# Attention with one more unit in flight, and two tiles that share the late slices at the head of three phases

## The chip, the cores and the metric

The kernel runs on one core of one Trainium2 chip, as one launch. The metric is device time in microseconds (us): the median of the runs of a kernel. Below, PE is TensorE (PEld its weight loads), DVE is VectorE, ACT is ScalarE, POOL is GpSimd, SP is the queue that issues the transfers.

## The reference

One inference step of a two-layer backbone, `D_MODEL` 1024, for 512 latent tokens and 128 context tokens that share one set of weights. Layer 0 mixes by attention (4 query heads, 2 key and value heads of 128) beside a Hyena convolution, layer 1 by a bidirectional mLSTM. Each layer ends with a gated ConvFFN of width 2816. Queries are taken in blocks of 128 rows. Around every sub-layer stand RMSNorm and a modulation whose vectors come from `w_mod`.

```python
def block_attention(q, k, v):
    ...
    s = jnp.einsum('bqkgd,bskd->bkgqs', qi, kf) * scale
    p = jax.nn.softmax(s, axis=-1)
    return jnp.einsum('bkgqs,bskd->bqkgd', p, vf)
...
def conv_ffn(x, w_up, conv_w, conv_b, w_down):
    h = dwconv3(x @ w_up, conv_w, conv_b)
    return (jax.nn.gelu(h[..., :D_FF], approximate=False) * h[..., D_FF:]) @ w_down
...
for l in range(DEPTH):
    ...
    xs = xs + mod_s[2] * rms_norm(out_s, norm_mix_post[l])
    hs = modulate(xs, norm_ffn_pre[l], mod_s[3], mod_s[4])
    ...
```

The outputs are the new token states of both groups, the new keys and values of the context, and the mLSTM states.

## The kernel before

The 640 tokens are five tiles of 128: tiles 0, 1, 2 are the first half (384 columns), tiles 3 and 4 the second (256). Every large product is made of three matmuls of float32 halves, a high part h and a low part l (`mm3`): h by h, l by h, h by l. So each activation slice has two tiles (`a1h`, `a1l`; `a3h`, `a3l` in the second ConvFFN) and each weight tile three: the raw one from the transfer (`wr`), the high part cast by ACT (`wh`) and the rest subtracted by DVE (`wl`). There are three buffers of `wh` and `wl`. A weight tile is 128 output columns by 1024, that is eight slices of the contraction (`KT` = 8), so a slice on one half is three matmuls.

The order of the instructions on every engine is fixed when the program is built. A planner (`Order`, `od`) keeps a model of every engine; generators for side work are spawned with a lead, and the main list of tasks takes a step of them where its model finds room. `od.until` waits in the model until operands are there, `od.take` and `od.gave` count PSUM tiles. There are three PSUM tiles of 1024 columns ("mm") and two of 512 ("aux").

**The head of a phase** (`fm_head`, from line 447). A phase's activations come from the residual stream by norm, transposes and casts, eight slices one after the other. The first five weight tiles of a phase do the first half of the tokens (`early`), the later halves follow (`late`, in the rows `g00l`, `g10l`). Two early tiles share one PSUM tile, under one name in the rows. In the rows `u` at the start of a ConvFFN is the PSUM tile of specs 3 and 4: its weights are w33 and w34 in the first ConvFFN and w165 and w166 in the second. Tile 1 of a phase does slices 0 to 7 and waits for each, then tile 2 does slices 0 to 7. In the second ConvFFN slices 4 to 7 are still being made when tile 1 starts; their casts run on ACT, DVE and POOL (`o1p0nt` is the transpose, `o1p0ny` the modulated slice). The same boundary then makes the slices of the second half (`o1p3...`), while tile 3 and its successors run. The mLSTM phase has the same head with its own specs.

**Attention** (`attend`, from line 1455). A unit is a block i of 128 query rows and one head (kv head kv, one of its two query heads a): `s` holds the scores (512 new keys and 128 cached ones) in a PSUM tile "mm", DVE takes the maximum `mx`, ACT the exponential `p` with its sum, DVE the reciprocal `rr` and the scaling of p; PE transposes p in five pieces into another "mm" tile `pt`, which ACT copies to SBUF; PE multiplies by the values into an "aux" tile `po`, which ACT copies to `mx`h, the mixer's output page. There are 20 units; the four with i = 4 are the context's and have one key block instead of five. A unit may start when all but the three ahead of it have ended. In between, the last pieces of the Hyena convolution (`iy`, `iz`), of the key and query transposes (`qkt`) and, on DVE, the sums of `w_mod` (`acc`<-`mw`) are worked on. The output projection follows (`o`, weights w25 to w32).

Of the kernel before, what the change touches and what calls it, by code (L numbers as in the profile page):

```python
# [15 lines left out]
ALU = mybir.AluOpType  # L16
AX = mybir.AxisListType

P = 128
# [306 lines left out]
def hybrid_step(ctx: ExitStack, tc: tile.TileContext, A: dict, O: dict):  # L326
# [18 lines left out]
    def page(name, dt=F32):  # L345
        return pp.tile([P, 648], dt, tag="pg", name=name)
# [85 lines left out]
    def fm_task(src, act, name, evac, needs=()):  # L432
# [11 lines left out]
                yield  # L444
        return Task(run, src)

    def fm_head(specs, act, needs_a, needs_b):


        n_ = len(specs)  # L450
        specs = specs[3:] + specs[:3]
        st, left = {}, {}

        def early(n):
            def run(w):
                if n % 2 == 0:
                    od.take("mm")
                    st[n] = mm(specs[n][1])
                    left[n] = min(2, n_ - n)
                st[n, "w"] = w  # L460
                o = n % 2 * 512
                yield from fm_part(st[n - n % 2][:, o : o + CUT], w, act, 0, CUT, needs_a if n == 0 else None)
                if EVF:
                    yield
            return Task(run, specs[n][0], hold=n >= n_ - 3)

        def late(n):
            def run(w):
                m, o = n - n % 2, n % 2 * 512
                own = OWN and n == n_ - 1 and not o  # L470
                if own:
                    pl = st[m][:, 512:1024]
                else:
                    od.take("aux")
                    pl = aux(specs[n][1] + "l")
                held = w is None
                yield from fm_part(pl[:, 0 : T - CUT], st[n, "w"] if held else w, act, CUT, T,
                                   needs_b if n == back[0] else None)
                if held and RB:
                    if EVF:  # L480
                        yield
                    release()
                specs[n][2]([(st[m][:, o : o + CUT], 0, CUT), (pl[:, 0 : T - CUT], CUT, T)])
                if not own:
                    od.gave("aux", pl)
                left[m] -= 1
                if not left[m]:
                    od.gave("mm", st[m])
                if held and not RB:
                    release()  # L490
            return Task(run, None if n >= n_ - 3 else specs[n][0])

        back = list(range(max(0, n_ - 3), n_)) + list(range(max(0, n_ - 3)))
        return [early(n) for n in range(n_)] + [late(n) for n in back]
# [596 lines left out]
    def forward(src, cols, out, name):  # L1091
# [21 lines left out]
            diff.append(t)  # L1113
            yield
        (c, s), (dc, ds) = sums, diff
        for o, x, y, op in ((out[0][:, a], c[:, a], c[:, b], ALU.add), (out[0][:, b], c[:, a], c[:, b], ALU.subtract),
                            (out[1][:, a], s[:, a], s[:, b], ALU.add), (out[1][:, b], s[:, b], s[:, a], ALU.subtract),
                            (out[2][:, a], dc[:, a], ds[:, b], ALU.add),
                            (out[2][:, b], dc[:, a], ds[:, b], ALU.subtract),
                            (out[3][:, a], dc[:, b], ds[:, a], ALU.subtract),  # L1120
                            (out[3][:, b], dc[:, b], ds[:, a], ALU.add)):
            nc.vector.tensor_tensor(o, x, y, op=op)
        yield

    def filters():
        z, w = hy["z"], hy["w"]
# [160 lines left out]
    def long_conv(hf):  # L1287
# [15 lines left out]
        HYE.tensor_tensor(yp[:, h1], vp[:, h0], gi, op=ALU.mult)  # L1303
        nc.vector.tensor_tensor(vp[:, h0], vp[:, h1], gi, op=ALU.mult)
        HYE.tensor_tensor(vp[:, h1], vp[:, h1], gr, op=ALU.mult)
        nc.vector.tensor_tensor(yp[:, h0], yp[:, h0], vp[:, h0], op=ALU.subtract)
        nc.vector.tensor_tensor(yp[:, h1], yp[:, h1], vp[:, h1], op=ALU.add)
        yield
# [5 lines left out]
        for n in range(2):  # L1314
# [2 lines left out]
            HYE.tensor_tensor(x[1], S, gs, op=ALU.mult)  # L1317
            nc.vector.tensor_tensor(C, C, gs, op=ALU.mult)
            HYE.tensor_tensor(S, S, gc, op=ALU.mult)
            nc.vector.tensor_tensor(x[0], x[0], x[1], op=ALU.subtract)  # L1320
            nc.vector.tensor_tensor(C, C, S, op=ALU.add)
            pl, mi = page(f"vp{n}{hf}")[:, 0:512], page(f"vm{n}{hf}")[:, 0:512]
            a, b = slice(0, 256), slice(256, 512)

# [101 lines left out]
        od.ready.add(("qk", i))  # L1426

    scale = DH ** -0.5

    def scores(kv, i, a):  # L1430
        h, nm = 2 * kv + a, f"{2 * kv + a}{i}"
# [18 lines left out]
    def attend():  # L1450
# [31 lines left out]
        def unit(n, u):  # L1482
            kv, i, a = u
            nk = 5 if i < 4 else 1
            yield [("qk", j) for j in (range(4) if i < 4 else (4,))] + [("at", j) for j in range(n - 3)]
            yield "mm"
            p, su, rr = scores(*u)
            yield
            nc.vector.reciprocal(rr, su)
            nc.vector.tensor_scalar(p, p, rr, None, op0=ALU.mult)  # L1490
            yield
            yield "mm"
            transposed(u, p)
            yield
            yield "aux"
            values(u)
            od.ready.add(("at", n))
# [553 lines left out]
    def release(away=False):  # L2051
        state["live"] -= not away
        issue(state["split"] + state["raws"])
        prefetch()
# [217 lines left out]
```

## Time and profile before

| | |
|---|---|
| runs | 1753.57, 1753.31, 1750.95 us; median 1753.31 |
| the profiled execution's own time | 1750.03 us |
| its span | 1748.1 us |
| busy: PE, PEld | 1686.0 (96%), 1524.9 (87%) |
| busy: DVE, ACT, POOL | 1246.7 (71%), 747.0 (43%), 354.2 (20%) |
| mean granted clock of PE, as a share of full speed | 0.986 |
| HBM over the span | 114 GB/s |

The times in the rows are microseconds from the start of the span of one profiled execution. Busy is the time in which an engine had an instruction under way; PE's matmuls overlap, so that the distance of their starts is the better measure of what one costs. "Idle before" is how long an engine stood still ahead of a row, and "<-" names what was last to release it.

### The profile page before, as it was taken

How to read it: one execution, taken by the hardware profiler on the slowest of the kernel's cores; microseconds unless marked ns; L12 is line 12 of the kernel's file. 1: busy time of each engine (PE TensorE's matmuls, PEld its weight loads, DVE VectorE, ACT ScalarE, POOL GpSimd, SP SyncE). 2: the span in 40 equal slices, each digit the busy share in tenths (PEclk: the TensorE clock that was granted, in tenths of full speed). 3: DMA queues.
4: the chain of work that ended last, by engine and by line, in shares of the span. 5: the costliest groups of instructions: out<-in, count | busy, mean ns of one | idle time of the engine just before them, and what ended most of it. 6: DMA issues, size and time to landing. Idle time of an engine off the chain costs nothing. (4 is left out here: it accounts for less than half of the span.)

```text
span 1748.1 us, 25489 instructions
## 1 busy us (share of the span) xinstructions
PE 1686.0 (96%) x10074; PEld 1524.9 (87%) x10074; DVE 1246.7 (71%) x2057; ACT 747.0 (43%) x1233; POOL 354.2 (20%) x187
## 2 busy tenths in 40 slices
PE   7899998899999999999999999998999999999997
PEld 2678787779999999888899999996889999998886
DVE  4688796767878777987767888886578844445455
ACT  2422545545434344454555444334354422333343
POOL 0000121001546453431013211120014411111000
PEclk9999999999999999999999999998999999999999
DMA  9245122411434343463524212122114322223343
GB/s 344 103 151 169 46 90 100 138 68 61 160 132 144 133 145 125 157 214 121 181 93 147 71 55 80 59 70 100 49 63 155 121 73 76 81 73 109 125 160 125
DMA packets 64352, 203.85 MB, mean 117 GB/s; under 512 B 7335, under 2 KB 12455, under 8 KB 64234
## 3 DMA queue, kind: packets, MB, share of 16 engines
q1 hardware_dynamic: 64234, 202.23, 33.9%
q8 instruction: 79, 1.29, 0.3%
q14 instruction: 39, 0.32, 0.1%
HBM read 196.17 MB, written 3.94 MB: 114 GB/s over the span
## 5 line engine op out<-in xcount | busy, mean ns | idle before, releaser
L284 DVE TENSOR_TENSOR wl<-wr,wh 128x1024 fp32r<-128x1024 f32 (+1 forms) x260 | 317.4, 1225 | 111.1 <-ACT wh L284 111.0
L284 ACT CAST wh<-wr 128x1024 fp32r<-128x1024 f32 (+1 forms) x260 | 263.5, 1018 | 151.6 <-PE dn L365 108.1
L284 DVE SCALAR_TENSOR_TENSOR acc<-mw,sc,acc 128x1024 f32<-128x1024 f32 x91 | 169.8, 1883 | 3.9 <-DMA mw<-in_w_mod 3.6
L284 POOL TENSOR_TENSOR hid<-zg,zu 128x640 f32<-128x640 f32 x44 | 105.9, 2408 | 321.7 <-DVE zu L284 317.9
L284 POOL TENSOR_TENSOR acc<-acc,modp 128x1024 f32<-128x1024 f32 x49 | 146.1, 2981 | 115.2 <-ACT modp L284 91.1
L284 DVE SCALAR_TENSOR_TENSOR zg<-g,vec,zg 128x127 f32<-128x127 f32 (+3 forms) x168 | 87.4, 541 | 93.2 <-ACT zg L284 90.2
L365 PE MATMUL dn<-wh,hh 128*128 128x512 f32 x440 | 139.3, 397 | 1.8 <-DVE zu L284 1.6
L365 PE MATMUL dn<-wl,hh 128*128 128x512 f32 x440 | 138.2, 394 | 0.0
L365 PE MATMUL dn<-wh,hl 128*128 128x512 f32 x440 | 138.2, 394 | 0.0
L284 DVE SCALAR_TENSOR_TENSOR zu<-u,vec,zu 128x511 f32<-128x511 f32 (+2 forms) x164 | 86.7, 549 | 62.8 <-ACT zu L284 59.9
L284 ACT ACTIVATE zu<-u,vec 128x640 f32<-128x640 f32 (+1 forms) x42 | 36.8, 876 | 174.3 <-PE u L365 174.3
L365 PE MATMUL u<-a3h,wh 128*128 128x384 f32 (+1 forms) x336 | 104.8, 312 | 2.9 <-DVE a3h L284 1.5
L365 PE MATMUL u<-a3l,wh 128*128 128x384 f32 (+1 forms) x336 | 105.0, 313 | 0.3 <-POOL a3l L284 0.3
L365 PE MATMUL u<-a3h,wl 128*128 128x384 f32 (+1 forms) x336 | 104.7, 312 | 0.2 <-DVE wl L284 0.2
L365 PE MATMUL u<-a1l,wh 128*128 128x384 f32 (+1 forms) x336 | 104.4, 311 | 0.5 <-POOL a1l L284 0.5
L365 PE MATMUL g<-a1h,wh 128*128 128x384 f32 (+1 forms) x336 | 104.8, 312 | 0.0
L365 PE MATMUL u<-a1h,wh 128*128 128x384 f32 (+1 forms) x336 | 104.6, 311 | 0.1
L365 PE MATMUL g<-a3h,wh 128*128 128x384 f32 (+1 forms) x336 | 104.4, 311 | 0.0
L365 PE MATMUL u<-a1h,wl 128*128 128x384 f32 (+1 forms) x336 | 104.0, 310 | 0.2 <-DVE wl L284 0.2
L365 PE MATMUL g<-a3l,wh 128*128 128x384 f32 (+1 forms) x336 | 104.2, 310 | 0.0
L365 PE MATMUL g<-a1l,wh 128*128 128x384 f32 (+1 forms) x336 | 104.2, 310 | 0.0
L365 PE MATMUL g<-a3h,wl 128*128 128x384 f32 (+1 forms) x336 | 104.1, 310 | 0.0
(742 smaller groups left out, 4454.9 us busy)
## 6 DMA issues: line engine op xcount, KB each, us to landing
wr<-in_w_up SPq DMA_DIRECT2D x92, 512.0 KB, 3.3
wr<-in_w_down SPq DMA_DIRECT2D x82, 512.0 KB, 3.8
mw<-in_w_mod SPq DMA_DIRECT2D x80, 512.0 KB, 4.3
wr<-in_w_ml SPq DMA_DIRECT2D x34, 512.0 KB, 3.9
wr<-in_w_out SPq DMA_DIRECT2D x18, 512.0 KB, 3.9
wr<-in_w_in SPq DMA_DIRECT2D x13, 512.0 KB
wr<-in_w_u SPq DMA_DIRECT2D x12, 512.0 KB, 5.5
we<-in_w_mod SPq DMA_DIRECT2D x8, 512.0 KB, 8.0
```

The costliest lines, as they stand in the source:

```text
L284: r = f(*args, **kw)
L365: r = nc.tensor.matmul(out, lhsT, rhs, start=start, stop=stop)
```

## The change

Two parts change the order of the instructions, and no instruction is added or taken away.

In `attend` the distance after which a unit may start becomes a number, `ATW` = 4 where a literal 3 stood: a unit may start when all but the four ahead of it have ended.

In `fm_head` the first two tiles of a phase (`EM` = 2) do slices 0 to 4 (`EK` = 5) of tile 1, then 0 to 4 of tile 2, then 5 to 7 of tile 1, after which its weight buffer is released, then 5 to 7 of tile 2 and its release. The planner now waits for each slice of an early tile where it waited for two at once from the second tile on. `FINE` = 0 in the convolution's generators adds hooks that do nothing (left out below).

```diff
--- before.py
+++ after.py
@@ -444,6 +444,9 @@
                 yield
         return Task(run, src)
 
+    EM = 2
+    EK = 5
+
     def fm_head(specs, act, needs_a, needs_b):
 
 
@@ -452,17 +455,35 @@
         st, left = {}, {}
 
         def early(n):
+            m = EM if n < EM else 1
+
+            def part(i, w, ks):
+                o = i % 2 * 512
+                out = st[i - i % 2][:, o : o + CUT]
+                for k in ks:
+                    if i < EM:
+                        od.need([(*needs_a, k)])
+                    od.until(od.avail([x[:, k * P : (k + 1) * P] for x in w] + [x[:, 0:CUT] for x in act[k]]))
+                    mm3(out, [x[:, k * P : (k + 1) * P] for x in w], [x[:, 0:CUT] for x in act[k]], k == 0, k == KT - 1)
+                    if k % 2:
+                        yield
+
             def run(w):
                 if n % 2 == 0:
                     od.take("mm")
                     st[n] = mm(specs[n][1])
                     left[n] = min(2, n_ - n)
                 st[n, "w"] = w
-                o = n % 2 * 512
-                yield from fm_part(st[n - n % 2][:, o : o + CUT], w, act, 0, CUT, needs_a if n == 0 else None)
-                if EVF:
-                    yield
-            return Task(run, specs[n][0], hold=n >= n_ - 3)
+                if m == 1:
+                    yield from part(n, w, range(KT))
+                    return
+                yield from part(n, w, range(EK))
+                if n == m - 1:
+                    for i in range(m):
+                        yield from part(i, st[i, "w"], range(EK, KT))
+                        release()
+                yield
+            return Task(run, specs[n][0], hold=n >= n_ - 3 or m > 1)
 
         def late(n):
             def run(w):
...
@@ -1426,6 +1457,7 @@
         od.ready.add(("qk", i))
 
     scale = DH ** -0.5
+    ATW = 4
 
     def scores(kv, i, a):
         h, nm = 2 * kv + a, f"{2 * kv + a}{i}"
@@ -1482,7 +1514,7 @@
         def unit(n, u):
             kv, i, a = u
             nk = 5 if i < 4 else 1
-            yield [("qk", j) for j in (range(4) if i < 4 else (4,))] + [("at", j) for j in range(n - 3)]
+            yield [("qk", j) for j in (range(4) if i < 4 else (4,))] + [("at", j) for j in range(n - ATW)]
             yield "mm"
             p, su, rr = scores(*u)
             yield
```

On SP and POOL the order stays as it was. It moves on PE, DVE and ACT in the attention and in the three heads, and nowhere else.

**PE, start of the attention.** Rows with `s` are scores, `qkt` and `iz` leftovers of the keys and the convolution, `pt` transposes of p, `po` the product with the values (vv); the three digits are kv, i, a, those behind `s` the head and i. Before:

```order
L365 MATMUL s11_2232<-qkT4_1127,qkT1_1124 128x512
L365 MATMUL s11_2232<-kc_1129,qkT1_1124 128x128
L376 MATMUL qkt41_2245<-ident_86,qsq4_1816 128x128 x3
L376 MATMUL pt000_2252<-ident_86,p00_2192 128x128 x5
L365 MATMUL iz3_2262<-dftp_113,yp1_1544 128x128 x2
L376 MATMUL pt001_2269<-ident_86,p10_2202 128x128 x5
L376 MATMUL pt010_2297<-ident_86,p01_2219 128x128 x5
L365 MATMUL po000_2305<-pt000_2258,vv0_1131 128x128 x2
L365 MATMUL po000_2305<-pt000_2258,vv1_1132 128x128 x2
L365 MATMUL po000_2305<-pt000_2258,vv2_1133 128x128
L365 MATMUL s02_2313<-qkT4_1127,qkT0_1123 128x512
```

And now:

```order
L365 MATMUL s11_2232<-qkT4_1127,qkT1_1124 128x512
L365 MATMUL s11_2232<-kc_1129,qkT1_1124 128x128
L365 MATMUL s02_2245<-qkT4_1127,qkT0_1123 128x512
L365 MATMUL s02_2245<-kc_1129,qkT0_1123 128x128
L376 MATMUL qkt41_2255<-ident_86,qsq4_1816 128x128 x3
L376 MATMUL pt000_2262<-ident_86,p00_2192 128x128 x5
L365 MATMUL iz3_2272<-dftp_113,yp1_1544 128x128 x2
L376 MATMUL pt001_2279<-ident_86,p10_2202 128x128 x5
L376 MATMUL pt010_2287<-ident_86,p01_2219 128x128 x5
L365 MATMUL po000_2317<-pt000_2268,vv0_1131 128x128 x2
L365 MATMUL po000_2317<-pt000_2268,vv1_1132 128x128 x2
L365 MATMUL po000_2317<-pt000_2268,vv2_1133 128x128
```

The scores of the fifth unit, `s02`, have moved from behind the first values to behind `s11`, ahead of three transposes.

**PE, late part of the attention.** Before, from the scores of kv head 1 and block 2 on:

```order
L365 MATMUL s32_2617<-qkT5_1128,qkT3_1126 128x512
L365 MATMUL s32_2617<-kc_1129,qkT3_1126 128x128
L365 MATMUL po040_2627<-pt040_2601,vv2_1133 128x128
L365 MATMUL s23_2630<-qkT5_1128,qkT2_1125 128x512
L365 MATMUL s23_2630<-kc_1129,qkT2_1125 128x128
L365 MATMUL po041_2640<-pt041_2612,vv2_1133 128x128
L365 MATMUL s33_2643<-qkT5_1128,qkT3_1126 128x512
L365 MATMUL s33_2643<-kc_1129,qkT3_1126 128x128
L376 MATMUL pt120_2653<-ident_86,p22_2597 128x128 x5
L376 MATMUL pt121_2668<-ident_86,p32_2625 128x128 x5
L376 MATMUL pt130_2678<-ident_86,p23_2638 128x128 x5
```

And now:

```order
L365 MATMUL s32_2601<-qkT5_1128,qkT3_1126 128x512
L365 MATMUL s32_2601<-kc_1129,qkT3_1126 128x128
L365 MATMUL s23_2613<-qkT5_1128,qkT2_1125 128x512
L365 MATMUL s23_2613<-kc_1129,qkT2_1125 128x128
L376 MATMUL pt040_2623<-ident_86,p04_2547 128x128
L376 MATMUL pt041_2629<-ident_86,p14_2572 128x128
L376 MATMUL pt120_2638<-ident_86,p22_2592 128x128 x5
L365 MATMUL po040_2648<-pt040_2625,vv2_1133 128x128
L365 MATMUL s33_2651<-qkT5_1128,qkT3_1126 128x512
L365 MATMUL s33_2651<-kc_1129,qkT3_1126 128x128
L365 MATMUL po041_2661<-pt041_2631,vv2_1133 128x128
L365 MATMUL s24_2664<-qkT5_1128,qkT2_1125 128x128
```

The scores of a unit stand one or two groups further ahead of its transposes: between `s22` and `pt120` stand now `s32` and `s23`, where `po040`, `po041` and `s33` stood as well before, and `s33` and `s24` come ahead of `pt121`.

**PE, head of the second ConvFFN.** `u11` is the PSUM tile of the first two weights, wh165 with wl165 and wh166 with wl166; the digit behind a3h and a3l is the slice. Before:

```order
L365 MATMUL u11_11739<-a3h4_11701,wh165_11609 128x384
L365 MATMUL u11_11739<-a3h4_11701,wl165_11610 128x384
L365 MATMUL u11_11739<-a3l4_11702,wh165_11609 128x384
L365 MATMUL u11_11739<-a3h5_11717,wh165_11609 128x384
L365 MATMUL u11_11739<-a3h5_11717,wl165_11610 128x384
L365 MATMUL u11_11739<-a3l5_11718,wh165_11609 128x384
L365 MATMUL u11_11739<-a3h6_11743,wh165_11609 128x384
L365 MATMUL u11_11739<-a3h6_11743,wl165_11610 128x384
L365 MATMUL u11_11739<-a3l6_11744,wh165_11609 128x384
L365 MATMUL u11_11739<-a3h7_11771,wh165_11609 128x384
L365 MATMUL u11_11739<-a3h7_11771,wl165_11610 128x384
L365 MATMUL u11_11739<-a3l7_11772,wh165_11609 128x384
```

And now:

```order
L365 MATMUL u11_11739<-a3h4_11701,wh165_11609 128x384
L365 MATMUL u11_11739<-a3h4_11701,wl165_11610 128x384
L365 MATMUL u11_11739<-a3l4_11702,wh165_11609 128x384
L365 MATMUL u11_11739<-a3h0_11631,wh166_11679 128x384
L365 MATMUL u11_11739<-a3h0_11631,wl166_11680 128x384
L365 MATMUL u11_11739<-a3l0_11632,wh166_11679 128x384
```

The slices 5 to 7 of the first weight stand behind slices 0 to 4 of the second now, at the end of this stretch:

```order
L365 MATMUL u11_11739<-a3h4_11701,wh166_11679 128x384
L365 MATMUL u11_11739<-a3h4_11701,wl166_11680 128x384
L365 MATMUL u11_11739<-a3l4_11702,wh166_11679 128x384
L365 MATMUL u11_11739<-a3h5_11717,wh165_11609 128x384
L365 MATMUL u11_11739<-a3h5_11717,wl165_11610 128x384
L365 MATMUL u11_11739<-a3l5_11718,wh165_11609 128x384
L365 MATMUL u11_11739<-a3h6_11743,wh165_11609 128x384
L365 MATMUL u11_11739<-a3h6_11743,wl165_11610 128x384
L365 MATMUL u11_11739<-a3l6_11744,wh165_11609 128x384
L365 MATMUL u11_11739<-a3h7_11774,wh165_11609 128x384
L365 MATMUL u11_11739<-a3h7_11774,wl165_11610 128x384
L365 MATMUL u11_11739<-a3l7_11775,wh165_11609 128x384
```

Fifteen matmuls of the second weight moved ahead of the nine of slices 5 to 7 of the first.

**ACT, head of the second ConvFFN.** `o1p3t3` and `o1p3t4` are the second half's residual tiles, whose squares are summed; wh168 and wh169 are the casts of the third and the fourth further weight. Before:

```order
L284 CAST wh168_11807<-wr168_11613 128x1024
L284 ACTIVATE o1p3t3_11736,o1p3nss_11800<-x3_2283 128x1024
L284 ACTIVATE o1p3t4_11762,o1p3nss_11800<-x4_2285 128x1024
L284 ACTIVATE o1p3t4_11762<-x4_2285,o1p3ny_11827 128x512 x2
L284 CAST wh169_11852<-wr169_11683 128x1024
L284 CAST a3h0_11631<-o1p3ny0_11874 128x256
```

And now:

```order
L284 CAST wh168_11829<-wr168_11613 128x1024
L284 ACTIVATE o1p3t3_11736,o1p3nss_11818<-x3_2303 128x1024
L284 CAST wh169_11842<-wr169_11683 128x1024
L284 ACTIVATE o1p3t4_11762,o1p3nss_11818<-x4_2305 128x1024
L284 ACTIVATE o1p3t4_11762<-x4_2305,o1p3ny_11867 128x512 x2
L284 CAST a3h0_11631<-o1p3ny0_11910 128x256
```

The cast of wh169 moved from behind the second half's scaling to between the two sums of squares.

## Rows read from the trace of the kernel before

**Rows 1.** Windows: attention, part of it, two heads (columns in line 1)

```profile
core 0: us, PE busy (x) PEld busy (x) DVE busy (x) ACT busy (x) POOL busy (x), PEclk, DMA share, GB/s
272.93:331.39 58.46, 48.29 (x318) 39.78 (x316) 40.96 (x88) 31.68 (x82) 4.02 (x3) 0.94 0.18 60
305.00:310.00 5.00, 3.16 (x15) 3.19 (x16) 3.57 (x8) 1.61 (x4) 0.00 (x0) 0.69 0.32 105
873.37:881.78 8.41, 8.41 (x49) 8.40 (x48) 7.93 (x17) 4.01 (x6) 0.00 (x0) 1.00 0.42 141
1264.92:1279.35 14.43, 11.22 (x55) 9.82 (x54) 12.34 (x25) 7.63 (x13) 2.04 (x2) 0.88 0.19 67
```

**Rows 2.** Timeline of PE in the attention: start, us, instruction, count

```profile
290.01 0.71 PE L376 MATMUL pt<-ident,p 128*128 128x128 f32 x5
290.55 1.02 PE L365 MATMUL s<-qkT,qkT 128*128 128x512 f32 x2
...
291.63 1.28 PE L365 MATMUL po<-pt,vv 128*128 128x128 f32 x10
292.75 1.02 PE L365 MATMUL s<-qkT,qkT 128*128 128x512 f32 x2
```

**Rows 3.** The same view, three waits [idle before <-releaser] and what follows them

```profile
306.84 1.24 PE L376 MATMUL pt<-ident,p 128*128 128x128 f32 x5 [1.97 <-DVE rr L284]
307.88 2.34 PE L365 MATMUL po<-pt,vv 128*128 128x128 f32 x10
...
319.34 1.39 PE L376 MATMUL pt<-ident,p 128*128 128x128 f32 x10 [1.31 <-DVE rr L284]
320.57 1.28 PE L365 MATMUL po<-pt,vv 128*128 128x128 f32 x10
...
327.00 0.30 PE L376 MATMUL pt<-ident,p 128*128 128x128 f32 x1 [1.92 <-DVE p L284]
...
331.39 0.71 PE L365 MATMUL o<-wh,o0h 128*128 128x512 f32 x2
```

**Rows 4.** Timeline of DVE and ACT in the attention: maximum, exponential, copies

```profile
296.23 0.82 DVE L284 TENSOR_REDUCE mx<-s 128x1 f32<-128x640 f32 x1 [1.19 <-PE s L365]
...
297.36 0.79 ACT L284 ACTIVATE p<-s,mx 128x640 f32<-128x640 f32 x1 [1.18 <-DVE rr L284]
...
298.15 2.03 ACT L284 COPY pt<-pt 128x640 f32<-128x640 f32 x3
```

**Rows 5.** Timeline of DVE, then of PE, behind the attention: three waits

```profile
332.49 1.29 DVE L284 TENSOR_TENSOR wl<-wr,wh 128x512 fp32r<-128x512 f32 x2 [1.66 <-ACT wh L284]
...
352.27 4.87 DVE L284 SCALAR_TENSOR_TENSOR acc<-mw,sc,acc 128x1024 f32<-128x1024 f32 x4 [2.64 <-DMA mw<-in_w_mod]
...
367.98 0.71 PE L365 MATMUL o<-wh,o0h 128*128 128x512 f32 x2 [0.62 <-DVE o0p0t L284]
```

**Rows 6.** Timeline of PE at the head of the first ConvFFN

```profile
395.61 0.34 PE L365 MATMUL u<-a1h,wh 128*128 128x384 f32 x1
...
398.73 0.34 PE L365 MATMUL u<-a1h,wh 128*128 128x384 f32 x1
...
417.80 0.39 PE L365 MATMUL g00l<-a1h,wh 128*128 128x256 f32 x1 [0.37 <-DVE o0p3ny L284]
```

**Rows 7.** Timeline of PE, second ConvFFN head, then a row of DVE

```profile
1267.96 0.34 PE L365 MATMUL u<-a3h,wh 128*128 128x384 f32 x1
...
1270.07 0.45 PE L365 MATMUL u<-a3h,wh 128*128 128x384 f32 x1 [1.42 <-ACT a3h L284]
...
1272.61 0.47 PE L365 MATMUL u<-a3h,wh 128*128 128x384 f32 x1 [1.51 <-DVE a3h L284]
...
1273.68 0.69 PE L365 MATMUL u<-a3l,wh 128*128 128x384 f32 x1 [0.28 <-POOL a3l L284]
1274.17 0.53 PE L365 MATMUL u<-a3h,wh 128*128 128x384 f32 x1
...
1277.60 1.22 DVE L284 TENSOR_TENSOR wl<-wr,wh 128x1024 fp32r<-128x1024 f32 x1
```

More of the change, by code (lines that the diff above doesn't have):

```diff
@@ L1115, in forward @@
         (c, s), (dc, ds) = sums, diff
-        for o, x, y, op in ((out[0][:, a], c[:, a], c[:, b], ALU.add), (out[0][:, b], c[:, a], c[:, b], ALU.subtract),
+        for n, (o, x, y, op) in enumerate(((out[0][:, a], c[:, a], c[:, b], ALU.add), (out[0][:, b], c[:, a], c[:, b], ALU.subtract),
                             (out[1][:, a], s[:, a], s[:, b], ALU.add), (out[1][:, b], s[:, b], s[:, a], ALU.subtract),
@@ L1120, in forward @@
                             (out[3][:, a], dc[:, b], ds[:, a], ALU.subtract),
-                            (out[3][:, b], dc[:, b], ds[:, a], ALU.add)):
+                            (out[3][:, b], dc[:, b], ds[:, a], ALU.add))):
             nc.vector.tensor_tensor(o, x, y, op=op)
+            if FINE and n % FINE == FINE - 1:
+                yield 0
         yield
+    FINE = 0
     def filters():
@@ L1305, in long_conv @@
         HYE.tensor_tensor(vp[:, h1], vp[:, h1], gr, op=ALU.mult)
+        if FINE:
+            yield 0
         nc.vector.tensor_tensor(yp[:, h0], yp[:, h0], vp[:, h0], op=ALU.subtract)
@@ L1319, in long_conv @@
             HYE.tensor_tensor(S, S, gc, op=ALU.mult)
+            if FINE:
+                yield 0
             nc.vector.tensor_tensor(x[0], x[0], x[1], op=ALU.subtract)
             nc.vector.tensor_tensor(C, C, S, op=ALU.add)
+            if FINE:
+                yield 0
             pl, mi = page(f"vp{n}{hf}")[:, 0:512], page(f"vm{n}{hf}")[:, 0:512]
```

## The prediction, made before the changed kernel ran

> **What bounds the kernel now.** I read the clock and busy shares first, then the windows around the four places whose order changes, then TensorE's own timeline there, and last the rows of the engines that its waits name. Over the whole span TensorE is nearly always busy, so an edit pays only where TensorE stands still, and only if the time is not waited again further on. The windows say where [rows 1]: the attention stretch lasts 58.46 us with TensorE busy 48.29, and its clock is 0.94; the head of the mLSTM phase is busy 8.41 of 8.41, so nothing can be won there; the head of the second ConvFFN is busy 11.22 of 14.43 at a clock of 0.88.
>
> In the attention (rows of 128 queries, one head: a unit) a full unit costs TensorE 1.08 us of scores, 0.54 of transposes and 1.12 of values, 2.74 together (differences of the starts in [rows 2]; 292.75 starts the next scores). From the first row that moves (272.93) to the output projection (331.39) there are 12 score groups, 16 transposes and 16 value groups of that size, 12.96 + 8.64 + 17.92 = 39.5 us, four small units (2.2, one key block instead of five) and two leftovers of the Hyena part (about 0.9), 42.6 in all. So 58.46 - 42.6, about 15.9 us, are lost. The waits are of one kind: transposes that wait for VectorE to scale p, 1.31 us three times (one of them stands in [rows 3]), then 1.97 and 1.92. Behind each of the two long ones the engine also ran at half speed: the ten value matmuls took 2.34 us at 307.88 and 1.28 elsewhere [rows 2, 3], and the granted clock of 305 to 310 is 0.69 [rows 1], a mixture of the two levels, 1.2 and 2.4 GHz. I put that at about 1.5 us for each of the two.
>
> Why p is late: after a score group VectorE takes the maximum (0.82), ScalarE the exponential (0.79), VectorE the reciprocal and the scaling, each queued behind the neighbours' work [rows 4]; ScalarE needs 2.03 for three copies of transposed tiles. With handovers a unit's chain is some 3 us, and with three earlier units unfinished TensorE has less than that of other work to put before it.
>
> **Change, attention.** Every operation stays; only the order moves. Each unit may start with four earlier ones unfinished, so its scores come about one group earlier on TensorE (s02 stands right behind s11), so 1.08 us more of work lies between a unit's scores and its transposes. The waits that this removes are the 1.31s, 1.97, 1.92, the small ones and the two half-speed stretches. What it adds: all scores and transposes take turns in three PSUM tiles. A score tile is held from the first matmul to the end of the exponential, 1.08 + 0.82 + 0.79 and some 0.2 between them, 2.9 us, a transposed one 0.54 + 0.68 (a third of 2.03), 1.25 [rows 2, 4]. That is 4.15 us a unit, over three tiles 1.38, half the 2.74 that TensorE needs: there are enough tiles on average, and only the order of the turns can make one late. I walked the new order row by row with the old durations. pt010 now waits for s02's exponential, whose maximum stands behind that of s11: s02 ends 1.08 after s11, its tile is free 2.1 later at the earliest (0.82 + 0.79 and some 0.5 of short steps), and 1.9 of other work lies between; with the two scalings of p that VectorE does first it is about 1.35 late. po000 waits 0.65 for a copy that stands behind an exponential, pt041 0.7, pt120 about 1.25, and pt131's copy stands behind the casts of the first output weight on ScalarE: 1.45. Five small ones (0.15 to 0.43) give 1.7. Sum 7.1, to 7.6 with the handovers. The longest is 1.45; 1.31 left the clock alone (the values after it took 1.28 at 320.57) and 1.92 did not [rows 3], so I forecast it full. 15.9 - 7.6 = 8.3: TensorE reaches the output projection some 8 us earlier.
>
> Not all of this is carried on. The next long wait is VectorE's: after the attention come the projection's weight residue (332.49) and later the sums with w_mod, which wait 2.64 us for a transfer at 352.27, and at 367.98 TensorE waits for the projection's result to be worked on by VectorE [rows 5]. That chain, not TensorE, then sets the time. In the new order three sums of 1.22 us (4.87 for four) stand between the last scaling and the second weight's residue, where two stood; by the walk the residue starts at about 325.45 instead of 332.49. **7.0 us** earlier is what I carry, with 4 (a third of the turns later than walked, or both half-speed stretches back) and 8.3 as ends. The transfer at 352.27 is issued behind weight loads whose buffers come free as TensorE goes on, so it moves along.
>
> A rule stands against this. The Trainium skill (Perfetto Trace Analysis, Optimization Strategy) says that a gap that repeats on the engine that should be full can mean that there is too little PSUM for the next tile. Here the rows name VectorE's p, not a tile, as what ended the repeated gap; by the rule one more unit would only move the gap to the tile and the attention would give nothing. That is rival A.
>
> **Change, first ConvFFN head.** Tile 1 and 2 of the phase now do slices 0 to 4 each, then 5 to 7 of the first, then of the second. A slice is three matmuls, 0.525 us (8.41 us for the 48 of two tiles, 0.175 each [rows 1]). Slice 5 starts at 395.61; nine matmuls without waiting would end at 397.19, and tile 2 starts at 398.73 [rows 6]: 1.54 us are lost on late slices. In the new order 2.6 us of tile 2's matmuls lie there, more than the 1.54 by which the last slice is late, so the loss goes. At the end of the head the second half's transposes were late too, 0.37 on g00l at 417.80 after some small delays; the new order does the VectorE chain for them about a microsecond earlier. **2.05 us** by the walk (1.54 + 0.5), ends 0 and 2.2. The price: tile 1's weight is released when its late slices are done, and the next cast starts then. By the walk the residues of the third and fourth weight still have 2.0 us or more in hand.
>
> **Change, mLSTM head.** Nothing to win [rows 1]: **0**, plus or minus 0.3 for a slice that is met a little sooner.
>
> **Change, second ConvFFN head.** Tile 1's slices 0 to 4 are done at 1267.96, where slice 5 starts [rows 7]. Slice 6 waits 1.42 us (1270.07), slice 7 1.51 (1272.61), its low part 0.28 more (1273.68), tile 2 starts at 1274.17, at half speed at first (0.53 us a matmul and not 0.34), and the third tile at 1279.35 [rows 1, 7]. In the new order 15 matmuls of tile 2 run from 1267.96 to 1270.58, slices 5 and 6 of tile 1 (both operands there by 1270.7) to 1271.63, slice 7 still waits for its operand at 1272.61 (1.0) and for the low part at 1273.68 (0.7), then nine matmuls of tile 2 end at 1275.43: 3.9 earlier than 1279.35. The half-speed stretch goes with it, as the two new waits are shorter than the old. The order on ScalarE puts the cast of wh169 ahead of the second squares of the residual, which makes that chain 1.1 later; the transposes that need it now stand behind the fourth tile, at 1275.43 + 8.4 = 1283.8, and find it done. At the first matmul of the second halves I find **4.1 us**; ends 1.5 (the half-speed stretch stays, and the next weight is late) and 4.3. The margin is thin: the next weight's residue was ready at 1278.8 (1277.60 + 1.22) [rows 7], the order ahead of it on VectorE is the old one, and it is now needed at 1275.43 + 4.2 = 1279.6, 0.8 later.
>
> **Sum.** 7.0 + 2.05 + 0 + 4.1 = 13.1 us. Behind the two heads TensorE is the bound again, and their gains go through. The profiled execution took 1750.03, so 1737 for one like it; it stands 3.3 under the median of the runs shown, 1753.31, on which the forecast is made: 1740.2, put at **1740.5**.
>
> **Rivals.** A: the attention gives almost nothing, because the turns of the three tiles or the w_mod chain hold it (a tile that is late twice as often as walked; for it the 2.64 wait on a transfer, against it the 1.37 us of 2.74). Then 2.05 + 4.1 to 2 more: -6 to -8, 1745 to 1747.5. Chance 0.17. B: the walk is right in kind, but one or two new waits near 1.4 us bring half speed back at 1.5 each: -10 to -11.5, 1742 to 1743.5; it lies within the forecast's own range (1735 to 1744), whose chance with it is 0.62. C: the later release makes the heads' next weights late and the heads give nothing; it decides when VectorE slips over 0.8 us in the second ConvFFN and 2 in the first: -7, 1746.3, 0.08. D: nothing measurable changes (both A and C, or the time is waited again before the end): 1750 to 1756.5, 0.09. E, the other side: TensorE falls to the lower level for the whole attention, as the shorter bursts between more frequent waits don't bring it up again. A half-speed stretch of 3.2 us costs 1.5, so nine of some fifteen such stretches eat the 13 us and more make it slower: with all of them -13 + 22, 1762. The rows speak against it: after 1.31 us of waiting the values ran at full speed [rows 3]. 0.04.
>
> A page bears on E: the Trainium skill (TensorE: Matmul & The Clock Gate, Part 4 PE-mode transpose) says that transposes don't count as busy like matmuls, and the new order brings transposes of several units closer together. No row here separates the two; by the rule E would be likelier than the 0.04 that the rows give it.
>
> **How the numbers follow.** The likeliest is the forecast with B, 1740.5. The range takes its lower end from all upper bounds (8.3 + 2.2 + 0.3 + 4.3 = 15.1, and some 3 of the spread between executions): 1735; its upper end takes in A and C: 1749. Outside remain D and E, and some 0.05 at the two edges. A measurement of this kernel can tell 0.2%, 3.5 us, from no change: faster 0.62 + 0.17 + 0.08 = 0.87; same 0.09; slower 0.04.
>
> **What would show it.** Right: no wait of over 1.5 us on TensorE between 273 and 323, the clock 0.98 or more there, the output projection at about 323, VectorE's second residue at about 325.5, tile 3 of the first ConvFFN head 1.5 sooner behind its phase's start and that of the second 3.9. Wrong: waits of transposes that name ScalarE's exponential of over 2 us, a clock under 0.9, the w_mod wait growing by what the attention won, or weight residues as releasers of the third and fourth tile of a head.

## The result, and the profile of the changed kernel

The changed kernel took 1737.08 us (median of 4 runs, 1735.53 to 1739.15), the kernel before 1752.13 beside it (4 runs, 1746.85 to 1753.57). The ratio is 0.992, with a 95% interval of 0.9896 to 0.9944: 14 us less, between 10 and 18. The forecast was 1740.5, 12.8 under the median that it started from, in a range of 1735 to 1749.

The profiled execution took 1739.15 us, its span is 1737.3, against 1748.1 before. These are the windows of the changed kernel that answer to [rows 1]: the attention from the scores s11 to the output projection, the heads of the first ConvFFN, the mLSTM and the second ConvFFN up to their third tile, and one stretch of the mLSTM phase. Columns as there.

```profile
core 0: us, PE busy (x) PEld busy (x) DVE busy (x) ACT busy (x) POOL busy (x), PEclk, DMA share, GB/s
272.57:324.01 51.44, 46.35 (x322) 37.71 (x320) 39.30 (x89) 31.96 (x87) 4.04 (x3) 1.00 0.19 69
385.11:393.93 8.82, 8.82 (x55) 8.79 (x53) 7.65 (x18) 3.58 (x8) 1.72 (x2) 1.00 0.01 3
862.76:871.19 8.43, 8.43 (x50) 8.43 (x48) 7.94 (x17) 4.01 (x6) 0.00 (x0) 1.00 0.40 140
1256.80:1267.43 10.63, 9.34 (x54) 8.66 (x53) 8.69 (x20) 5.32 (x9) 2.04 (x2) 1.00 0.27 89
919.70:926.50 6.80, 6.80 (x29) 6.13 (x28) 1.61 (x2) 2.24 (x4) 0.00 (x0) 0.50 0.42 151
```

Of the kernel before, the window of the first ConvFFN's head, and s11 (timeline):

```profile
392.56:402.91 10.35, 9.78 (x54) 8.63 (x53) 9.16 (x19) 5.09 (x10) 1.73 (x2) 1.00 0.01 2
...
271.85 1.02 PE L365 MATMUL s<-qkT,qkT 128*128 128x512 f32 x2
```

The attention stretch was 59.54 us before (271.85 to 331.39, [rows 3]) and is 51.44, at a clock of 1.00. The first ConvFFN's head lasts 8.82 and lasted 10.35, the second's 10.63 after 14.43, the mLSTM's 8.43 after 8.41. The last row is not part of the change: here TensorE was at the lower level for a stretch in which the program has no new work, and the execution lost about 3 us to it: from the wait just ahead of that stretch to the second ConvFFN it needed 339.4 us, the kernel before 336.6 and a second profile of the changed kernel 336.0. That is most of why the two profiles differ by 10.9 us and not by 14.

These are all of TensorE's waits that the view marks in the attention now (timeline, start, duration, instruction, [idle before <- releaser]), with the start of the output projection:

```profile
278.14 0.76 PE L376 MATMUL pt<-ident,p 128*128 128x128 f32 x5 [1.07 <-DVE rr L284]
279.22 1.38 PE L365 MATMUL po<-pt,vv 128*128 128x128 f32 x10 [0.32 <-ACT pt L284]
...
298.25 0.77 PE L376 MATMUL pt<-ident,p 128*128 128x128 f32 x5 [0.48 <-ACT p L284]
...
311.08 0.33 PE L376 MATMUL pt<-ident,p 128*128 128x128 f32 x1 [0.91 <-ACT p L284]
312.37 0.77 PE L376 MATMUL pt<-ident,p 128*128 128x128 f32 x5 [0.96 <-ACT p L284]
...
321.64 1.60 PE L365 MATMUL po<-pt,vv 128*128 128x128 f32 x12 [0.84 <-ACT pt L284]
...
323.76 0.49 PE L365 MATMUL po<-pt,vv 128*128 128x128 f32 x2 [0.41 <-ACT pt L284]
324.01 0.71 PE L365 MATMUL o<-wh,o0h 128*128 128x512 f32 x2
```

In the order of the program these are pt010, po000, pt100, pt041, pt120, po131 and po141. Before there were nine, the five largest of 1.31 to 1.97 us; now none is over 1.07. In sum they were 10.17 us and are 5.00. The other 2.9 of the 8.1 us fit the two half-speed stretches, which are gone and were put at about 1.5 us each.

Behind the attention, VectorE's second residue, its wait for the w_mod transfer and TensorE's wait for VectorE, as in [rows 5]:

```profile
325.81 1.29 DVE L284 TENSOR_TENSOR wl<-wr,wh 128x512 fp32r<-128x512 f32 x2
...
344.75 4.87 DVE L284 SCALAR_TENSOR_TENSOR acc<-mw,sc,acc 128x1024 f32<-128x1024 f32 x4 [1.56 <-DMA mw<-in_w_mod]
...
360.46 0.70 PE L365 MATMUL o<-wh,o0h 128*128 128x512 f32 x2 [0.60 <-DVE o0p0t L284]
```

In the kernel before TensorE had one more wait there, for a part that VectorE makes from the sums with w_mod:

```profile
358.53 0.50 PE L365 MATMUL modp<-modb,onesr 128*128 128x512 f32 x1 [0.23 <-DVE modb L284]
```

And the heads, as in [rows 6] and [rows 7]:

```profile
393.93 0.34 PE L365 MATMUL g<-a1h,wh 128*128 128x384 f32 x1
...
408.28 0.38 PE L365 MATMUL g00l<-a1h,wh 128*128 128x256 f32 x1
...
1264.46 0.44 PE L365 MATMUL u<-a3h,wh 128*128 128x384 f32 x1 [0.80 <-DVE a3h L284]
...
1265.56 0.44 PE L365 MATMUL u<-a3l,wh 128*128 128x384 f32 x1 [0.49 <-POOL a3l L284]
...
1267.43 0.33 PE L365 MATMUL g<-a3h,wh 128*128 128x384 f32 x1
...
1282.38 0.38 PE L365 MATMUL g10l<-a3h,wh 128*128 128x256 f32 x1 [0.66 <-ACT o1p3ny L284]
...
1285.95 0.39 PE L365 MATMUL g10l<-a3l,wh 128*128 128x256 f32 x1 [0.30 <-POOL a3l L284]
1286.17 0.28 PE L365 MATMUL u10l<-a3h,wh 128*128 128x256 f32 x1
```

The second halves of the second ConvFFN in the kernel before:

```profile
1295.07 0.28 PE L365 MATMUL g10l<-a3h,wh 128*128 128x256 f32 x1
...
1297.89 0.28 PE L365 MATMUL u10l<-a3h,wh 128*128 128x256 f32 x1
```

Here 393.93 and 1267.43 are the third tiles, 408.28 and 1282.38 the first matmuls of the second halves. Against the kernel before, the program stood at +0.72 us at s11 (a difference from ahead of the change), at -7.38 at the output projection, -7.52 at 360.46, -8.98 at the first ConvFFN's third tile, -9.52 at its g00l (408.28 for 417.80), -8.12 at the start of the second ConvFFN (1256.80 for 1264.92, the lower clock in between), and -11.72 at u10l (1286.17 for 1297.89).

### The profile page after: what moved, and what is told of

It is laid out like the page before. It is cut to its first block, busy times and chain, and to the rows that moved or that the text cites. A ratio compares the mean times of both kernels' runs of the same rounds, so it can differ in the third digit from the quotient of the medians.

```text
span 1737.3 us, 25489 instructions
## 1 busy us (share of the span) xinstructions
PE 1683.4 (97%) x10074; PEld 1523.0 (88%) x10074; DVE 1243.6 (72%) x2057; ACT 746.3 (43%) x1233; POOL 353.8 (20%) x187
## 5 line engine op out<-in xcount | busy, mean ns | idle before, releaser
L365 PE MATMUL g<-a1h,wl 128*128 128x384 f32 (+1 forms) x336 | 104.0, 310 | 0.0
```

What stands on the lines that cost most here:

```text
L365: r = nc.tensor.matmul(out, lhsT, rhs, start=start, stop=stop)
```

## The experiments

**The two parts apart, and together.** In the first kernel the heads do one tile after the other (`EM` = 1), in the second the attention keeps its distance of 3; the third is the changed kernel again, on the same chip.

```diff
-    EM = 2
+    EM = 1
```

> Only the attention's distance is 4; the heads do their tiles one after the other as before. Theory (more work ahead of each unit's transposes removes the waits for p, and the chain through VectorE and the w_mod transfer carries it on): 7 to 8.5 us under the kernel before, output projection 8 us earlier counted from the scores of the fourth unit (s11), no half-speed stretch in the attention. Rival 1 (the gain is the absence of two half-speed stretches that the one profile of before happened to show): 5 us under. Rival 2 (the w_mod chain gives the time back): under 4 us.

```diff
-    ATW = 4
+    ATW = 3
```

> Only the heads share their late slices; the attention keeps 3. Theory: 2.05 us from the head of the first ConvFFN, 3.6 to 4.1 from that of the second, nothing from the mLSTM head: 5.5 to 6.2 us under the kernel before. Rival (weights released later make the next tiles wait, or the gain is returned before the next phase): 0 to 2 us under.

> The changed kernel again, for the sum on the same chip. Theory (the two parts lie far apart and add up): the gain of the attention alone plus that of the heads alone within 1.5 us, 13 to 15 us under the kernel before. Rival (they share a limit behind them): less than the sum by 3 us or more.

The attention alone: ratio 0.9949 (0.9933 to 0.9966), 8.9 us under 1751.74 (6.0 to 11.7), where 7 to 8.5 were expected. The heads alone: 0.9966 (0.9953 to 0.998), 6.0 us (3.5 to 8.2). Both: 0.9934 (0.9914 to 0.9953), 11.6 us (8.2 to 15.1), under the 13 to 15 that were expected. The sum of the two is 14.9; 11.6 is 3.3 less, and the first measurement of the same kernel gave 14. With intervals this wide the times neither show nor exclude a shared limit. The profiles are sharper: from s11 to the output projection the attention takes 51.44 us with the attention alone and 51.43 with both, 59.53 with the heads alone; the heads up to the third tile take 8.81 and 10.60 with the heads alone, 8.82 and 10.62 with both. Neither part touches the other's stretch.

With the heads alone the attention has the waits and both lower-clock stretches of the kernel before, at the same places of the program (timeline of TensorE, then windows, in the run with the heads alone):

```profile
304.88 1.23 PE L376 MATMUL pt<-ident,p 128*128 128x128 f32 x5 [1.97 <-DVE rr L284]
325.03 0.30 PE L376 MATMUL pt<-ident,p 128*128 128x128 f32 x1 [1.92 <-DVE p L284]
325.68 2.93 PE L365 MATMUL po<-pt,vv 128*128 128x128 f32 x12 [0.35 <-ACT pt L284]
...
305.00:308.40 3.40, 3.40 (x16) 3.37 (x16) 1.68 (x4) 0.82 (x2) 0.00 (x0) 0.50 0.51 154
```

The values behind the 1.92 take 2.93 us here, where the changed kernel needs 1.60. So the two half-speed stretches of [rows 1] and [rows 3] were no chance of one execution, and rival 1 of the attention alone falls. Rival 2 (the w_mod chain gives the time back) falls by the median. But the profiled execution of the attention alone shows how it could look. Its transfer landed 7.5 us after its issue at 340.81, where that of the changed kernel took 4.3 (340.47 to 344.75):

```profile
348.29 4.87 DVE L284 SCALAR_TENSOR_TENSOR acc<-mw,sc,acc 128x1024 f32<-128x1024 f32 x4 [4.76 <-DMA mw<-in_w_mod]
...
353.10 0.50 PE L365 MATMUL modp<-moda,onesr 128*128 128x512 f32 x1 [1.77 <-ACT moda L284]
354.54 0.80 PE L365 MATMUL modp<-modb,onesr 128*128 128x512 f32 x1 [0.95 <-DVE modb L284]
...
353.60:360.40 6.80, 5.86 (x14) 4.61 (x15) 3.19 (x4) 2.02 (x2) 0.00 (x0) 0.50 0.00 0
```

TensorE waited 1.77 and 0.95 us for the parts made from w_mod, and then ran at the lower level. From the output projection to the start of the ConvFFN that execution needed 66.6 us, the changed kernel 61.1. This is not tied to the new order. Of the profiled executions of this case, those with a distance of 4 needed 61.1 to 61.6 us four times and 64.0 to 66.6 three times. Those with 3 needed 60.9 and 61.2 and, with the heads alone, 64.6, where VectorE waited 4.01 us for the transfer. Whether the new order makes it likelier, so few executions do not show.

**One more in flight still.**

```diff
-    ATW = 4
+    ATW = 5
```

> The changed kernel with the distance 5 in place of 4. Theory (with 4 the waits left are those for turns of the three score and transpose tiles, named by ScalarE's exponential, so scores that come still earlier only hold tiles longer): 0 to 4 us above the changed kernel, waits of scores and transposes on ScalarE's p longer in sum than the 2.4 us of the changed kernel. Rival (p is still late and one more unit covers more of it): 2 to 4 us under the changed kernel.

The time does not tell it from the changed kernel: 0.9932 (0.9913 to 0.9951), where that has 0.9934 beside it. The stretch does: 53.57 us from s11 to the projection, 2.1 more than with 4.

```profile
276.70 0.77 PE L376 MATMUL pt<-ident,p 128*128 128x128 f32 x5 [0.71 <-ACT p L284]
...
280.57 0.77 PE L376 MATMUL pt<-ident,p 128*128 128x128 f32 x5 [0.86 <-ACT p L284]
...
295.61 0.76 PE L376 MATMUL pt<-ident,p 128*128 128x128 f32 x5 [0.94 <-ACT p L284]
...
308.05 0.33 PE L376 MATMUL pt<-ident,p 128*128 128x128 f32 x1 [0.57 <-ACT p L284]
...
321.13 0.30 PE L376 MATMUL pt<-ident,p 128*128 128x128 f32 x1 [1.92 <-DVE p L284]
```

The waits that name ScalarE's p, the exponential that frees a tile, are 0.71, 0.86, 0.94 and 0.57, in sum 3.1 us against the 2.35 of the changed kernel (0.48, 0.91, 0.96). That much was expected of tiles held longer. The rest, 1.92 us before the last small units and a half-speed stretch behind it (323.3 to 326.7), was not: the same wait stands at the tail of the order with 3. The Trainium skill (Perfetto Trace Analysis, Optimization Strategy) reads a repeated gap as a possible lack of PSUM for the next tile. For the gap of the kernel before that was not so, since its rows name VectorE and it was gone with a distance of 4 and the same three tiles; for the waits named p that are left with 4 and 5 (2.35 and 3.1 us) the traces agree.

**One less.**

```diff
-    ATW = 4
+    ATW = 2
```

> The changed kernel with the distance 2. Theory (each step of the distance is about one score group, 1.08 us, of cover for each transpose): the stretch from s11 to the output projection 64 to 75 us, against 59.5 with 3 and 51.4 with 4, with waits named rr of 2 us and more and more than two half-speed stretches; 1755 to 1770 us. Rival (the step from 3 to 4 removed a single bad place in the order and not a shortage all along): 58 to 62 us.

1752.11 us in one run, and 62.28 us from s11: both under what was expected (1755 and 64), and 62.28 just above what the rival allows. The yardstick was a poor one: with a distance of 2, s11 itself has to wait, and starts at 276.83. From the first scores to the projection it is 72.35 us with 2 (266.76 to 339.11), 65.00 with 3 (266.39 to 331.39), 56.90 with 4 (267.11 to 324.01) and 59.03 with 5. So the steps from 2 to 3 and from 3 to 4 are worth 7.4 and 8.1 us, and the one run with 2 took 7.2 us more than the median with the heads alone, whose distance is 3 (1744.93). So the two steps have about the same price, by a yardstick that was chosen after the result. The waits are not those expected (named rr, 2 us and more), and there are two half-speed stretches (318 to 322 and 332 to 339), not more. The longest waits are for copies at the end of the attention:

```profile
318.56 0.79 PE L365 MATMUL po<-pt,vv 128*128 128x128 f32 x2 [2.15 <-ACT pt L284]
...
331.15 1.57 PE L365 MATMUL po<-pt,vv 128*128 128x128 f32 x10 [2.63 <-ACT pt L284]
```

**A shorter chain, same order.** VectorE's maximum reads 128 of a unit's 640 scores, once with the order of distance 3 and once with that of 4. It leaves out four fifths of the maximum, and the exponent is scaled down; the lines for that, and those that keep the planner's model and so the order, are left out here.

```diff
-        nc.vector.tensor_reduce(mx, s, axis=AX.X, op=ALU.max)
+        nc.vector.engine.tensor_reduce(mx, s[:, 0:P], axis=AX.X, op=ALU.max)
...
```

> Distance 3 in the attention with the heads as changed, and VectorE's maximum reads 128 of a unit's 640 score columns (0.29 us in place of 0.82; the softmax exponent is scaled down so that it stays finite); the order of every engine is that of the run with the heads alone. Theory (the waits named rr are for a chain of maximum, exponential and scaling that is longer than the work ahead of the transposes): each of the waits 0.87, 1.31 three times and 1.97 falls by 0.5 us or more, the stretch from the scores s11 to the output projection from 59.5 to 54.5 to 57 us, the half-speed stretch behind the 1.97 goes; the 1.92 near the end, behind a small unit, stays. Rival (tiles or ScalarE set the pace): the stretch falls by less than 1 us.

```profile
272.61 0.68 PE L365 MATMUL iz<-dftp,yp 128*128 128x128 f32 x4 [0.45 <-DVE rr L284]
...
282.59 1.40 PE L376 MATMUL pt<-ident,p 128*128 128x128 f32 x10 [0.78 <-DVE rr L284]
...
303.44 0.74 PE L376 MATMUL pt<-ident,p 128*128 128x128 f32 x5 [1.97 <-DVE rr L284]
...
320.89 0.30 PE L376 MATMUL pt<-ident,p 128*128 128x128 f32 x1 [1.93 <-DVE p L284]
...
303.44:306.84 3.40, 3.40 (x25) 2.92 (x26) 2.19 (x7) 0.96 (x2) 0.00 (x0) 1.00 0.51 154
```

One run took 1738.49 us. The stretch fell from 59.54 to 54.93 us. The waits of 1.31 are 0.78, all three, by exactly the 0.53 that the maximum is shorter; 0.87 became 0.45. The 1.97 did not move, against the expectation: it stands behind a small unit's maximum, which always had 128 columns, and a sum with w_mod on VectorE. The half-speed stretch behind it was gone all the same in this one execution, while that behind the 1.93 near the end stayed.

> The changed kernel with the same shorter maximum (128 of 640 columns, exponent scaled down), order unchanged. Theory (what is left of the waits hangs on the same chain, now through the tile that the exponential frees): the waits 1.07, 0.48, 0.91 and 0.96 fall by 0.3 to 0.5 each, the 0.84 and 0.41 for copies near the end stay, the stretch from s11 to the output projection goes from 51.4 to 49.3 to 50.2 us. Rival (what is left are copies and turns that a faster chain does not touch): 51 us or more.

```profile
276.68 0.77 PE L376 MATMUL pt<-ident,p 128*128 128x128 f32 x5 [0.31 <-DVE rr L284]
...
308.35 0.33 PE L376 MATMUL pt<-ident,p 128*128 128x128 f32 x1 [0.38 <-ACT p L284]
309.40 0.77 PE L376 MATMUL pt<-ident,p 128*128 128x128 f32 x5 [0.73 <-ACT p L284]
...
318.14 1.60 PE L365 MATMUL po<-pt,vv 128*128 128x128 f32 x12 [0.84 <-ACT pt L284]
```

One run took 1733.04 us. 51.44 us became 48.33, below the expected 49.3 to 50.2: 1.07 fell to 0.31, 0.48 went, 0.91 fell to 0.38 and 0.96 to 0.73, and the waits for copies (0.84 here) stayed. The marked waits fell by 2.0 us of the 3.1; the rest the view does not mark. The chain of maximum, exponential and scaling is what TensorE waits for in both orders; with 4 it is less of it.

**The late slices in turn.** Slices 5, 6 and 7 are done for both tiles before the next slice begins.

```diff
-                    for i in range(m):
-                        yield from part(i, st[i, "w"], range(EK, KT))
-                        release()
+                    for k in range(EK, KT):
+                        for i in range(m):
+                            yield from part(i, st[i, "w"], (k,))
+                            if k == KT - 1:
+                                release()
```

> The changed kernel with the late slices taken in turn: 5 of both tiles, 6 of both, then 7 of both. Theory (in the second ConvFFN head only slice 7 is still late, by 0.80 and 0.49 us): the third tile starts 1.0 us sooner, 9.6 us after the phase's start in place of 10.63; in the first ConvFFN head nothing changes (8.82); at the second halves' second tile (u10l) the gain is gone, as the chain for the second half is then late. Rival 1: the gain is kept there, 28.3 us from the phase's start in place of 29.37. Rival 2 (nothing, the slice is waited for all the same): 10.6.

```profile
1268.99 0.44 PE L365 MATMUL u<-a3l,wh 128*128 128x384 f32 x1 [0.45 <-POOL a3l L284]
...
1284.26 0.39 PE L365 MATMUL g10l<-a3h,wh 128*128 128x256 f32 x1 [0.26 <-DVE o1p3ny L284]
...
1288.64 0.38 PE L365 MATMUL g10l<-a3h,wh 128*128 128x256 f32 x1 [0.39 <-DVE a3h L284]
...
1289.44 0.38 PE L365 MATMUL g10l<-a3l,wh 128*128 128x256 f32 x1 [0.30 <-POOL a3l L284]
```

The third tile starts 9.55 us after the phase's start, 1.08 sooner, and u10l 29.42 after it, where the changed kernel has 29.37; the first ConvFFN's head has 8.83 for 8.82. The gain is gone at u10l, as expected. The rows name the second half's slices, which the same engines make next: g10l starts 1.6 us sooner (24.01 us after the phase's start, for 25.58), and its 24 matmuls, with the transposes between them, then take 5.4 us in place of 3.8. The one run took 1743.04 us; its profile has the lower clock in the mLSTM phase and 64.5 us between the projection and the ConvFFN, so the time says nothing of this change.

**The planner's waits.** The run with the attention alone had 14.36 us from the first ConvFFN's third tile to g00l, though its shared slices were off; the kernel before has 14.89. What was left of the change there is that the planner waits for each slice of an early tile, not for two at once. So two more kernels: the kernel before with nothing but the distance 4, and the changed kernel with the wait for two from the third tile on.

```diff
-[("at", j) for j in range(n - 3)]
+[("at", j) for j in range(n - 4)]
```

> The kernel before with the attention's distance 4 and nothing else: the heads' code is untouched, also the planner's waits for two slices at once in the later tiles of a head. Theory (the run with the attention alone had a second difference, the wait for each slice, which puts the second half's transposes earlier): stretch from s11 to the output projection 51.4 us as there; from the third tile to g00l 14.9 us as in the kernel before and not 14.36; 6 to 9 us under the kernel before. Rival (the 0.53 us between those two was chance): 14.36 again.

```diff
-                    od.until(od.avail([x[:, k * P : (k + 1) * P] for x in w] + [x[:, 0:CUT] for x in act[k]]))
+                    if i < EM:
+                        od.until(od.avail([x[:, k * P : (k + 1) * P] for x in w] + [x[:, 0:CUT] for x in act[k]]))
+                    elif k % 2 == 0:
+                        od.until(od.avail([x[:, k * P : (k + 2) * P] for x in w] + [x[:, 0:CUT] for x in act[k] + act[k + 1]]))
```

> The changed kernel, but from the third tile of a head on the planner waits for two slices at once again, as before; the shared late slices of the first two tiles stay. Theory: third tile to g00l 14.7 to 14.9 us in place of 14.35, with a wait for o0p3ny back; in the second ConvFFN, where the chain of the second half is the limit anyway, the third tile to u10l within 0.6 us of 18.75. Rival (the 0.5 us come from the shared slices, whose VectorE chain is earlier): 14.35 as now.

```profile
413.09 0.38 PE L365 MATMUL g00l<-a1h,wh 128*128 128x256 f32 x1 [0.37 <-DVE o0p3ny L284]
...
408.65 0.39 PE L365 MATMUL g00l<-a1h,wh 128*128 128x256 f32 x1 [0.36 <-DVE o0p3ny L284]
```

Both have 14.90 us, and the wait for o0p3ny is back in both (0.37 and 0.36, in the order of the two edits). In the second ConvFFN, from the third tile to u10l, the last kernel needs 18.64 us and the changed one 18.74. The half microsecond belongs to the finer wait, which lets the second half's transposes go ahead one slice sooner. The attention with nothing else gave 0.9946 (0.9924 to 0.9968), 9.5 us under 1751.59, with 51.42 us from s11; the other kernel took 1736.04 us in its one run.

## Why the prediction held, point by point

**The attention's losses.** The sum was 15.9 us of lost time against 7.6 in the new order. Of the 51.44 us, 1.08 are s11 and 42.6 work, so 7.8 are lost. The waits came where the walk had put them: pt010 1.07 (walked 1.35), po000 0.32 (0.65), pt041 0.91 (0.7), pt120 0.96 (1.25), po131 behind pt131's copy 0.84 (1.45). Four of the five name what was expected, p and the copies. That of pt010 names rr, but the scaling of its own p had ended at 277.76; s02's exponential, which the walk had there, ended at 277.99, 0.15 us ahead of the transposes. That the sum came within 0.2 us is partly luck: these five were 5.4 us in the walk and 4.1 in the trace, and the small waits and handovers, put at 2.2, are 3.7.

**What is carried on.** This is the step that failed. The text said that VectorE's chain with w_mod, not TensorE, sets the time behind the attention, and carried 7.0 us of 8.3. VectorE's second residue did start at 325.81, where 325.45 was said. But TensorE has no marked wait from the projection at 324.01 to 360.46, where it waits 0.60, as it waited 0.62 before; it reached that point 7.52 us earlier, and counted from s11 8.24. In this execution all of the attention's gain was carried. The row at 352.27 was a wait of VectorE: whether TensorE stood still for it had to be read from TensorE's rows, and they had no wait to show but 0.23 at 358.53 and 0.62. The chain is close behind, though. With a transfer that lands 3 us later, as in the run with the attention alone, TensorE waits for it, and so it does with the heads alone, at the old distance.

**First ConvFFN head.** 1.54 was said for the late slices, 1.53 came (10.35 to 8.82). The 0.5 at the end of the head came too (14.89 to 14.35), for another reason: I put it down to an earlier chain on VectorE, and the last two experiments show that it is the planner's finer wait, a part of the diff that I had passed over.

**mLSTM head.** 8.41 and 8.43: nothing, as said. Behind it the planner's finer wait gave 0.3 us that the walk did not have: from the phase's start to the end of the wait of 0.72 us that stands in it (0.73 before) the changed kernel takes 54.60 us, the kernel before 54.91 and the two kernels of the last experiment 54.92 and 54.93.

**Second ConvFFN head.** 3.9 at the third tile was said, 3.79 came, with the two waits left of 0.80 and 0.49 (1.0 and 0.7 said) and without the half-speed stretch. The 4.1 were said for the first matmul of the second halves. There, at g10l, it is 4.57 (25.58 us after the phase's start, for 30.15). But at u10l 3.60 are left: the second half's slices are late now (0.66 and 0.30 in the rows above), which the walk had as done in time. The weights' margin of 0.8 us held: up to the second halves no wait names a residue.

**Sum and rivals.** By the profile 8.2 + 2.0 + 0 + 3.6 = 13.8, where 7.0 + 2.05 + 0 + 4.1 = 13.1 was said; the two measurements gave 14 and 11.6. That the sum is so close is helped by two errors of opposite sign, 1.2 too little behind the attention and 0.5 too much at u10l. A fell (the attention gave 8), and so did C, D and E. B did not come: no wait near 1.4 us was left, and the clock of the stretch is 1.00. One reading under E was wrong: the new order does not bring transposes closer together. Before, 15 stood in a row three times; now it is at most 10. So the run says nothing of the rule that was named there.

## What to carry to other kernels

Where an engine waits again and again for the same chain of other engines, lay work of its own between the start of the chain and its use, and check in the new order what the deeper overlap holds longer: here three tiles were enough for a distance of 4, and with 5 the waits for them grew. A wait on a second engine counts only if the bound engine's own rows show that it stands still for it. And a gain at the start of a phase is worth what the next late operand leaves of it: one more microsecond at the third tile was gone twenty microseconds later.

## What the runs showed of the hardware

In the attention TensorE's clock stayed at 1.00 behind all eleven waits of 1.30 and 1.31 us, and fell to 0.50 behind eight of the nine of 1.92 to 2.63 us. The length of one wait does not decide it: behind the 1.97 the granted clock was 0.50 in the run with the heads alone (305.0 to 308.4), and it stayed at 1.00 behind the same 1.97 with the shorter chain and distance 3, where the waits ahead were half a microsecond shorter. That these are the cause is not shown by one execution: behind 1.77 and 0.95 us, the waits for the parts made from w_mod, the clock fell with the attention alone, and behind 1.76 and 0.96 at the same place it stayed at 1.00 in the kernel before with nothing but the distance 4.

Between 918 and 938 us, in the mLSTM phase, five of twelve profiled executions ran at half speed for 7 to 10 us, among them the changed kernel's (0.50 in the rows above), and seven did not. The wait just ahead of it was the same, 0.72 us in the changed kernel and 0.73 in its second profile, which kept the full clock there. From that wait to the second ConvFFN the five took 339.4 to 340.1 us, the seven 335.6 to 336.6: this place alone is worth 3 to 4 us between two executions.

The last transfers of w_mod ahead of the ConvFFN landed 4.3 us (changed kernel) to 7.5 us (attention alone) after their issue, with the same program around them. Of four executions in which VectorE waited over 4 us for them, three then had a half-speed stretch between 351 and 363.

One thing stays open. From g00l of the first ConvFFN to the mLSTM phase, 455 us of nearly gapless matmuls, six of the seven executions whose attention has the changed order took 454.5 us; the seventh, with the shorter maximum, and the five with another distance 455.5 to 456.1. Behind u10l the changed kernel is 0.9 us slower than the kernel before (451.11 and 450.25). TensorE's instructions are in the same order there. What differs was not tried.
